# Part of the second feed-forward product in seven block products instead of eight (Strassen's scheme)

## The chip, the cores and the metric

One Trainium2 chip, one core. The metric is the device time of one execution in microseconds (us). The kernel before has a median of 726.84 us over 3 runs (726.24 to 728.11).

## What is computed

A transformer block over 512 tokens of width 1024, all in float32: four gated branches, an output product, and a feed-forward part. The change touches only the last of these:

```python
h = rmsnorm(x, norm_ffn_pre[l])
f = jnp.square(jax.nn.relu(h @ w_ff1[l])) @ w_ff2[l]
x = x + rmsnorm(f, norm_ffn_post[l])
```

`w_ff1` is 1024 x 4096, `w_ff2` is 4096 x 1024. The second product therefore sums over 32 K tiles of 128 for each of 4 token tiles of 128 and each of 2 column halves of 512.

## The kernel before, in words

**Three matmuls for one.** Each operand of a float32 product is split in a high part, rounded to the engine's fp32r form, and a low part, the remainder. `mm3` (L138) issues high x high, high x low and low x high. Every split costs one pass of ACT (the cast to the high part) and one of DVE (the subtraction that leaves the low part). `split_w` (L115) does so for a weight tile of 128 x 1024 and gives it one of five `wh`/`wl` buffers; `load` (L110) brings the raw tile over SP's queue into one of three `raw` buffers; `weights` (L135) is both. `split_by_dma` (L122) makes the low part without DVE: ACT writes the negated high part, and a DMA from POOL's queue adds the raw tile to it from memory.

**Order.** PE's instructions are kept in the order in which the program is written (`InOrder`, L85 to L102). For the other engines and the DMA queues the framework's planner chooses the order before the run, from the order of the program and from when it expects operands and buffers. A buffer that a pool reuses makes its next writer wait for its last reader (`reuse_waits="tile"`: tile by tile, also where one pool takes the memory of another that was closed).

**First feed-forward product.** It is already done in seven block products per pair of K tiles: `seven_w` (L337) makes the weight sums, `seven` (L351) issues seven `part`s of 12 matmuls of 256 columns into banks pa to pd, `forms` (L385) are the halves and sums of `h`. The loop at L1003 runs over the pairs j = 4, 6, ... 30. `finish` (L971) squares the relu into `u[j]` and splits it (`usplit`, L950, three buffers).

**Second product, left column half.** Inside that loop `second()` (L963) takes a finished K tile from `pend` and adds it to the four banks `acc`: 12 matmuls of 512 columns. It stands once after the fifth of the seven parts, and once or more at the end of the iteration (`while pend`).

**Second product, right column half.** After the loop `acc2` is summed over all 32 K tiles (L1037 to L1049). The last `LAST` = 6 K tiles are split ahead into buffers of their own (`held`), and the tail (L1050) runs token tile by token tile: six K tiles, a square with its sum on ACT, `norm_scale`, three passes of DVE, and two output DMAs. The left half is scaled into `fo` before (L1028 to L1032), and `gpost` is loaded at L1026 into memory that the pools of `hs` (the halves and sums of `h`) held.

Of the kernel before, what the change touches and what calls it, by code (L numbers as in the profile page):

```python
# [10 lines left out]
F32 = mybir.dt.float32  # L11
F32R = mybir.dt.float32r
I32 = mybir.dt.int32
AF = mybir.ActivationFunctionType
ALU = mybir.AluOpType
# [3 lines left out]
P = 128  # L19
S = 512  # L20
NT = S // P
D = 1024
# [8 lines left out]
NFF = DFF // P  # L31
# [49 lines left out]
def build(ctx, tc, d, out):  # L81
    nc = tc.nc
    DVE, POOL = nc.vector, nc.gpsimd
# [18 lines left out]
    PE, ACT = InOrder(nc.tensor, True), InOrder(nc.scalar, False)  # L102

    def f(t):
        return t.bitcast(F32)
# [4 lines left out]
    def load(src, n=1024):  # L110
        raw = wp.tile([P, 1024], F32, tag="raw", name="raw", bufs=3)
        nc.sync.dma_start(raw[:, :n], src)
        return raw

    def split_w(raw, n=1024):  # L115
        hi = wp.tile([P, 1024], F32R, tag="wh", name="wh", bufs=5)
        lo = wp.tile([P, 1024], F32R, tag="wl", name="wl", bufs=5)
        ACT.copy(hi[:, :n], raw[:, :n])
        DVE.tensor_tensor(lo[:, :n], raw[:, :n], f(hi)[:, :n], ALU.subtract)  # L119
        return hi, lo  # L120

    def split_by_dma(src, raw=None, n=1024, own=None):  # L122

        raw = load(src, n) if raw is None else raw
        if own is None:
            hi = wp.tile([P, 1024], F32R, tag="wh", name="wh", bufs=5)
            lo = wp.tile([P, 1024], F32R, tag="wl", name="wl", bufs=5)
        else:
            hi, lo = [own.tile([P, 1024], F32R, tag=f"b{c}", name=f"b{c}", bufs=1) for c in "hl"]
        ACT.copy(hi[:, :n], raw[:, :n])  # L130
        ACT.activation(lo[:, :n], f(hi)[:, :n], AF.Copy, scale=-1.0)
        POOL.dma_start(lo[:, :n], src.bitcast(F32R), accum_op=ALU.add)
        return hi, lo

    def weights(src, n=1024):  # L135
        return split_w(load(src, n), n)

    def mm3(ps, lhs, rhs, start, stop, more=False):  # L138

        k = dict(skip_group_check=more)  # L140
        PE.matmul(ps, lhs[0], rhs[0], start=start, stop=False, **k)
        PE.matmul(ps, lhs[0], rhs[1], start=False, stop=False, **k)
        PE.matmul(ps, lhs[1], rhs[0], start=False, stop=stop, **k)

    def sl(pair, *ix):
        return pair[0][ix], pair[1][ix]
# [39 lines left out]
    def bank(name):  # L186
        return mm.tile([P, 512], F32, tag="mm", name=name)
# [96 lines left out]
    for (a, b), xt, wa in zip(groups, xts, was):  # L284
        if a == 1:
            angles = rope_tables()
        for k in range(a, b):
# [11 lines left out]
            for i, (zz, ww) in enumerate(((zh, wah), (zl, wah), (zh, wal))):  # L299
                for t in range(NT):  # L300
                    PE.matmul(psA[t][:, :NA], zz[:, k, t * P:(t + 1) * P], ww[:, k, :],
                              start=k == 0 and i == 0, stop=k == KD - 1 and i == 2)
# [34 lines left out]
    def seven_w(srcs, by_dma):  # L337

        left, rght = load(srcs[0]), load(srcs[1])
        w = split_w(left)  # L340
        w22 = split_by_dma(srcs[1][:, B2], rght[:, B2], 512) if by_dma else split_w(rght[:, B2], 512)

        DVE.tensor_tensor(left[:, B1], rght[:, B1], left[:, B1], ALU.subtract)
        DVE.tensor_tensor(rght[:, B1], rght[:, B2], rght[:, B1], ALU.subtract)
        DVE.tensor_tensor(rght[:, B2], rght[:, B2], left[:, B1], ALU.subtract)
        DVE.tensor_tensor(left[:, B2], left[:, B2], rght[:, B2], ALU.subtract)
        yield w, w22
        yield split_w(left)
        yield split_w(rght)

    def seven(ws_, forms, small, g, h):  # L351

        A11, A12, A22, S1, S2, S3, S4 = forms
        (w, w22), wl, wr = ws_
        pa, pb = bank("pa"), bank("pb")
        part(pa, w, 0, A11, True)
        x1 = small()
        ACT.copy(x1, pa[:, :HS])
        yield
        part(pb, w, 512, A12, True)  # L360
        DVE.tensor_tensor(g[:, :HS], pb[:, :HS], x1, ALU.add)
        yield
        pc = bank("pc")
        part(pc, wl, 0, S1, True)
        x5 = small()
        ACT.copy(x5, pc[:, :HS])
        yield
        part(pa, wr, 512, S2, False)
        x2 = small()
        ACT.copy(x2, pa[:, :HS])  # L370
        yield
        pd = bank("pd")
        part(pd, wl, 512, A22, True)
        yield
        part(pc, w22, 0, S4, False)
        DVE.tensor_tensor(h[:, :HS], pc[:, :HS], x2, ALU.add)
        yield
        part(pa, wr, 0, S3, False)
        x3 = small()
        ACT.copy(x3, pa[:, :HS])  # L380
        DVE.tensor_tensor(g[:, HS:], pd[:, :HS], x3, ALU.add)  # L381
        DVE.tensor_tensor(h[:, HS:], x3, x5, ALU.add)
        yield
# [556 lines left out]

    up = ctx.enter_context(tc.tile_pool(name="up", bufs=1, reuse_waits="tile", **right))

    u = [up.tile([P, S], F32, name=f"u{j}") for j in reversed(range(NFF))][::-1]
    sst = up.tile([P, TOP], F32, name="sst")[:, :4 * NT].rearrange("p (t c) -> p t c", c=4)
    us = ctx.enter_context(tc.tile_pool(name="us", bufs=3, reuse_waits="tile", **right))
    acc = [bank("acc") for _ in range(NT)]

    pend = []

    def usplit(j):  # L950
        uh = us.tile([P, S], F32R, tag="uh", name="uh")
        ul = us.tile([P, S], F32R, tag="ul", name="ul")
        ACT.copy(uh, u[j])
        DVE.tensor_tensor(ul, u[j], f(uh), ALU.subtract)  # L954
        return uh, ul

    def ff2(dst, j, w, us_, t, first=0, last=NFF - 1):
        mm3(dst[t], sl(us_, slice(None), slice(t * P, (t + 1) * P)), sl(w, slice(None), slice((j % 2) * 512, (j % 2 + 1) * 512)),
            j == first, j == last)

    w2 = {0: weights(d["w2"][0, 0])}

    def second():  # L963

        j, us_ = pend.pop(0)
        if j and j % 2 == 0:
            w2[0] = weights(d["w2"][0, j // 2])
        for t in range(NT):
            ff2(acc, j, w2[0], us_, t)

    def finish(j):  # L971
        ACT.activation(u[j], u[j], AF.Relu)
        ACT.activation(u[j], u[j], AF.Square)
        pend.append((j, usplit(j)))

    first = seven_w((d["w1"][EARLY], d["w1"][EARLY + 1]), False)
    first_w = [next(first)]
# [24 lines left out]
    ops = forms(h2, hsum)  # L1002
    for j in range(EARLY, NFF, 2):  # L1003
        g, h = u[j], u[j + 1]
        for n, _ in enumerate(seven(first_w if j == EARLY else list(seven_w((d["w1"][j], d["w1"][j + 1]), False)),
                                      ops, small, g, h)):
            if n == 4 or n in (1, 2) and j == EARLY:
                second()
        while pend:
            second()  # L1010
        if j == NFF - 2:
            ahead_u = usplit(0)
        finish(j)
        finish(j + 1)

    acc2 = [bank("acc2") for _ in range(NT)]
    w = weights(d["w2"][1, 0])
    for t in range(NT):
        ff2(acc2, 0, w, ahead_u, t)
    while pend:  # L1020
        second()
    hs.close()

    lp = ctx.enter_context(tc.tile_pool(name="lp", bufs=1, reuse_waits="tile"))
    gpost = lp.tile([P, D], F32, name="gpost")
    nc.sync.dma_start(gpost, d["gpost"].partition_broadcast(P))  # L1026
    fo = lp.tile([P, NT, 512], F32, name="fo")
    for t in range(NT):  # L1028
        sq = lp.tile([P, S], F32, tag="r", name="r", bufs=2)
        ACT.activation(sq, acc[t], AF.Square, scale=r2[:, t:t + 1], accum_out=sst[:, t, 0:1])  # L1030
        DVE.tensor_scalar(sst[:, t, 0:1], sst[:, t, 0:1], D * EPS, None, ALU.add)
        DVE.scalar_tensor_tensor(fo[:, t, :], acc[t], r2[:, t:t + 1], gpost[:, :512], ALU.mult, ALU.mult)  # L1032


    LAST = 6
    held = []
    for j in range(1, NFF):  # L1037
        if j % 2 == 0:
            w = weights(d["w2"][1, j // 2])
        us_ = usplit(j) if j < NFF - LAST else None  # L1040
        if us_ is None:
            uh = lp.tile([P, S], F32R, name=f"luh{j}")
            ul = lp.tile([P, S], F32R, name=f"lul{j}")
            ACT.copy(uh, u[j])
            DVE.tensor_tensor(ul, u[j], f(uh), ALU.subtract)
            held.append((j, w, (uh, ul)))
        else:
            for t in range(NT):
                ff2(acc2, j, w, us_, t)  # L1049
    for t in range(NT):  # L1050
        for j, w, us_ in held:
            ff2(acc2, j, w, us_, t)
        sq = lp.tile([P, S], F32, tag="r", name="r", bufs=2)
        f2 = lp.tile([P, D], F32, tag="f2", name="f2", bufs=2)
        ACT.activation(sq, acc2[t], AF.Square, scale=r2[:, t:t + 1], accum_out=sst[:, t, 1:2])
        norm_scale(sst[:, t, 2:3], sst[:, t, 3:4], sst[:, t, 0:1], sst[:, t, 1:2])
        DVE.scalar_tensor_tensor(f2[:, 512:], acc2[t], r2[:, t:t + 1], gpost[:, 512:], ALU.mult, ALU.mult)
        DVE.scalar_tensor_tensor(f2[:, :512], fo[:, t, :], sst[:, t, 2:3], x1[:, t, :512], ALU.mult, ALU.add)
        nc.sync.dma_start(out[t * P:(t + 1) * P, :512], f2[:, :512])
        DVE.scalar_tensor_tensor(f2[:, 512:], f2[:, 512:], sst[:, t, 2:3], x1[:, t, 512:], ALU.mult, ALU.add)  # L1060
        nc.sync.dma_start(out[t * P:(t + 1) * P, 512:], f2[:, 512:])
# [78 lines left out]
```

## Time and profile before

| | |
|---|---|
| median of 3 runs | 726.84 us (726.24 to 728.11) |
| the profiled execution, its own time | 727.39 us |
| its span in the trace | 725.7 us |
| granted TensorE clock, mean | 0.999 of 2.4 GHz |
| gates' stage (seven-product form, accumulating DMAs) | 215 to 331 us |
| loop of the first feed-forward product | 406 to 623 us |
| rest of the second product | 623 to 719 us |
| last output | 719 to 726 us |

The profile names the engines PE (TensorE matmul), PEld (weight loads, beside PE), DVE (VectorE), ACT (ScalarE), POOL (GpSimd) and SP (the queue of most DMAs). A busy time is the sum of the instructions' durations. A row of a group reads: line, engine, operation, output <- inputs, form, count | busy us, mean ns | idle time of the engine just before, and who ended it. The chain of waits goes back from the last instruction, at each step to what released it.

### The profile page before, as it was taken

The numbers are of one execution on the slowest core, as the hardware profiler recorded it, in microseconds if no ns is written. First come the engines' busy times: TensorE is split into PE (matmuls) and PEld (weight loads), VectorE is DVE, ScalarE is ACT, GpSimd is POOL, SyncE is SP. The second block draws the span as 40 slices with busy tenths as digits, with TensorE's granted clock in tenths as the row PEclk, the third lists the DMA queues.
The fourth block names the chain that finished last, engine by engine and source line by source line (L and its number), as shares of the span: only waits on it lengthen the run. The fifth ranks groups of instructions, "written<-read, shape, count | busy, mean of one in ns | idle before, by whom it ended". The sixth has DMA issues, their size and how long they took to land.

```text
span 725.7 us, 11480 instructions
## 1 busy us (share of the span) xinstructions
PE 715.5 (99%) x4490; PEld 646.0 (89%) x4490; DVE 532.4 (73%) x887; ACT 405.6 (56%) x681; POOL 31.4 (4%) x49
## 2 busy tenths in 40 slices
PE   8999999999999999999999999999999999999996
PEld 7998788888999999998889999999999999888885
DVE  7599986994788988887368977766776767764515
ACT  6875444564556666663446754656555566744411
POOL 1110000000100100100011000000000000000001
PEclk9999999999999999999999999999999999999999
DMA  8533221242447646658424133233332332633103
GB/s 305 192 111 117 88 88 59 88 117 73 114 108 187 141 113 154 148 158 295 135 68 143 59 112 92 89 122 112 93 111 89 108 121 91 203 102 102 59 1 116
DMA packets 26182, 86.71 MB, mean 119 GB/s; under 512 B 3344, under 2 KB 3856, under 8 KB 26128
## 3 DMA queue, kind: packets, MB, share of 16 engines
q1 hardware_dynamic: 23072, 78.12, 32.6%
q0 software_dynamic: 3056, 7.87, 6.5%
q8 instruction: 35, 0.57, 0.3%
q14 instruction: 19, 0.16, 0.1%
HBM read 83.87 MB, written 2.10 MB: 118 GB/s over the span
## 4 chain that ended last, share of the span: by engine, by line
PE 95%; DVE 3%; DMA 1%; issue 0%; SPq 0%; ACT 0%; DVEq 0%; ACTq 0%
PE acc L95 24%; PE pa L95 15%; PE fb L95 12%; PE pc L95 10%; PE y L95 6%; PE wo L95 6%; PE pb L95 5%; PE pd L95 5%; PE z L95 3%; PE psA L95 2%; PE sgv L95 2%; PE po L95 1%; DMA wA<-in_wA 1%; PE tr L95 1%; PE s L95 1%; PE q L95 1%
## 5 line engine op out<-in xcount | busy, mean ns | idle before, releaser
L95 ACT CAST wh<-raw 128x1024 fp32r<-128x1024 f32 (+2 forms) x171 | 165.8, 981 | 142.2 <-PE pc L95 54.9
L119 DVE TENSOR_TENSOR wl<-raw,wh 128x1024 fp32r<-128x1024 f32 (+2 forms) x157 | 181.8, 1169 | 34.8 <-ACT wh L95 32.5
L95 PE MATMUL acc<-wh,uh 128*128 128x512 f32 x232 | 90.6, 391 | 0.0
L95 PE MATMUL acc<-wl,uh 128*128 128x512 f32 x232 | 90.6, 391 | 0.0
L95 PE MATMUL acc<-wh,ul 128*128 128x512 f32 x232 | 90.4, 390 | 0.0
L954 DVE TENSOR_TENSOR ul<-u,uh 128x512 fp32r<-128x512 f32 x58 | 38.7, 689 | 58.2 <-ACT uh L95 58.2
L95 PE MATMUL fb<-zh,wh 128*128 128x512 f32 x144 | 56.7, 394 | 0.1
L95 PE MATMUL fb<-zl,wh 128*128 128x512 f32 x144 | 56.1, 390 | 0.0
L95 PE MATMUL fb<-zh,wl 128*128 128x512 f32 x144 | 56.1, 390 | 0.0
L95 ACT CAST uh<-u 128x512 fp32r<-128x512 f32 x58 | 34.2, 617 | 33.9 <-PE acc L95 33.7
L95 PEld LDWEIGHTS acc<-wh,ul 128*128 128x128 f32 x232 | 43.6, 188 | 9.8 <-DVE ul L954 0.4
L95 PEld LDWEIGHTS acc<-wh,uh 128*128 128x128 f32 x232 | 43.6, 188 | 8.7 <-ACT uh L95 0.4
L95 PEld LDWEIGHTS acc<-wl,uh 128*128 128x128 f32 x232 | 43.5, 188 | 7.8
L95 ACT ACTIVATE u<-u 128x512 f32<-128x512 f32 x60 | 33.1, 621 | 17.7 <-DVE u L381 17.7
L95 ACT COPY x<-pa 128x256 f32<-128x256 f32 x78 | 28.6, 367 | 9.9 <-PE pa L95 8.3
L95 PEld LDWEIGHTS fb<-zh,wl 128*128 128x128 f32 x144 | 27.0, 188 | 5.8
L95 PEld LDWEIGHTS fb<-zh,wh 128*128 128x128 f32 x144 | 27.1, 188 | 5.7 <-DVE zc L434 0.4
L95 PEld LDWEIGHTS fb<-zl,wh 128*128 128x128 f32 x144 | 27.1, 188 | 5.3
L95 PE MATMUL pa<-hsh,wh 128*128 128x256 f32 x112 | 31.2, 279 | 0.0
L95 PE MATMUL pa<-hsl,wh 128*128 128x256 f32 x112 | 31.2, 279 | 0.0
L95 PE MATMUL pa<-hsh,wl 128*128 128x256 f32 x112 | 31.2, 279 | 0.0
L95 ACT ACTIVATE g<-g,c 128x512 f32<-128x512 f32 x32 | 22.5, 720 | 9.7 <-DVE g L821 9.7
(391 smaller groups left out, 1995.0 us busy)
## 6 DMA issues: line engine op xcount, KB each, us to landing
raw<-in_w SPq DMA_DIRECT2D x64, 512.0 KB, 3.5
raw<-in_wG SPq DMA_DIRECT2D x32, 512.0 KB, 3.6
raw<-in_wF SPq DMA_DIRECT2D x10, 512.0 KB, 3.6
raw<-in_wB SPq DMA_DIRECT2D x8, 512.0 KB, 4.8
raw<-in_wO SPq DMA_DIRECT2D x8, 512.0 KB, 4.5
bl<-in_wB POOLq DMA_DIRECT2D x7, 512.0 KB, 7.7
wl<-in_wG POOLq DMA_DIRECT2D x12, 256.0 KB, 4.3
xk<-in_x SPq DMA_DIRECT2D x4, 512.0 KB, 8.6
```

What stands on the lines that cost most here:

```text
L95: ins = op(*a, **k)
L119: DVE.tensor_tensor(lo[:, :n], raw[:, :n], f(hi)[:, :n], ALU.subtract)
L954: DVE.tensor_tensor(ul, u[j], f(uh), ALU.subtract)
```

## The change

K tiles 20 to 31 leave the plain sum and are taken in three rounds of two pairs each: round m combines the pairs `K0[m]` (tiles 20 to 25) and `K1[m]` (26 to 31), the halves of the tokens (`TA`, `TB`) and the column halves. The seven products of a round are spread over three places: four in the left half (A11 B11 into `pa`; A12 B21 into `acc[:2]`; S1 T1 into `pc`; A22 T4 into `acc[2:]`), two in the right half (S2 T2 into `pa`; A22' with S4 into `pc`), and one near the end (S3 T3 into `pa`). `pc` goes on as the first half of `acc2`. Partial results are copied to `fix` and added at the end. Each round loads its weight tiles anew in each place; sums of weights and of tokens are made by DVE, and split.

In the loop of the first product only one `second()` is left per iteration, `todo` holds K tiles until one of two places in `pend` is free, and `seven_w` is called with its accumulating form (True). K tiles 0 to 15 are added in the loop, 16 to 19 (`KEEP`) during the left rounds. The `u` tiles are allocated in pairs. The pool `qp` (raw tiles, token halves) and later `ep` (the `held` buffers) lie in memory that was `hs`'s.

```diff
+    pairs_u = [up.tile([P, 2, S], F32, name=f"u{j}") for j in reversed(range(NFF // 2))][::-1]
+    u = [pairs_u[j // 2][:, j % 2, :] for j in range(NFF)]
...
+    DUOS = 3
+    WHOLE = NFF - 4 * DUOS
+    KEEP = 4
+    pend, todo = [], []
+
+    def refill():
+        while todo and len(pend) < 2:
+            j = todo.pop(0)
+            pend.append((j, usplit(j)))
...
-            ff2(acc, j, w2[0], us_, t)
+            ff2(acc, j, w2[0], us_, t, j == 0, j >= WHOLE - KEEP - 1, j >= WHOLE - KEEP)
+        refill()
...
-        pend.append((j, usplit(j)))
+        if j < WHOLE:
+            todo.append(j)
+            refill()
...
-        for n, _ in enumerate(seven(first_w if j == EARLY else list(seven_w((d["w1"][j], d["w1"][j + 1]), False)),
+        for n, _ in enumerate(seven(first_w if j == EARLY else list(seven_w((d["w1"][j], d["w1"][j + 1]), True)),
...
-        while pend:
-            second()
...
+    def temp():
+        return lp.tile([P, S], F32, tag="r", name="r", bufs=4)
...
+    def loadq(src):
+        raw = qp.tile([P, 1024], F32, tag="raw", name="rawq", bufs=3)
+        nc.sync.dma_start(raw, src)
+        return raw
+
+    def halves_of(v):
+
+        a, b = [qp.tile([P, S], F32R, tag=f"a{c}", name=f"a{c}", bufs=5) for c in "hl"]
+        ACT.copy(two(a), v)
+        DVE.tensor_tensor(two(b), v, f(two(a)), ALU.subtract)
+        return two(a), two(b)
+
+    def block(dst, a, w, first):
+
+        for k in range(2):
+            for t in range(2):
+                mm3(dst[t], sl(a(k), slice(None), slice(t * P, (t + 1) * P)), sl(w, slice(None), slice(k * 512, (k + 1) * 512)),
+                    first and k == 0, k == 1, not first)
...
+    for m in range(DUOS):
+        last = m == DUOS - 1
+        u0, u1 = K0[m], K1[m]
+        b11, b12 = load(d["w2"][0, c0_ + m]), load(d["w2"][1, c0_ + m])
+        w11 = split_by_dma(d["w2"][0, c0_ + m], b11) if m else split_w(b11)
+        DVE.tensor_tensor(b11, b12, b11, ALU.subtract)
+        a11 = halves_of(u0[:, :, TA])
+        for _ in range(1 if m else 2):
+            second()
+        block(pa, of(a11), w11, m == 0)
...
+        b21, b22 = loadq(d["w2"][0, c1_ + m]), loadq(d["w2"][1, c1_ + m])
+        w21 = split_by_dma(d["w2"][0, c1_ + m], b21) if m else split_w(b21)
+        both = [halves_of(two(u1[:, k, :])) for k in range(2)]
...
+        block(acc[:2], lambda k: flat(k, TA), w21, False)
...
+        wt1 = split_w(b11)
+        v = temp()
+        DVE.tensor_tensor(two(v), u0[:, :, TB], u1[:, :, TB], ALU.add)
+        s1_ = halves_of(two(v))
+        block(pc, of(s1_), wt1, m == 0)
...
+        DVE.tensor_tensor(b22, b22, b11, ALU.subtract)
+        DVE.tensor_tensor(b21, b21, b22, ALU.subtract)
+        wt4 = split_w(b21)
+        block(acc[2:], lambda k: flat(k, TB), wt4, False)
...
+    for m in range(DUOS):
+        u0, u1 = K0[m], K1[m]
+        for _ in range(3 if m < 2 else 2):
+            third()
+        b11, b12 = load(d["w2"][0, c0_ + m]), load(d["w2"][1, c0_ + m])
+        b22 = loadq(d["w2"][1, c1_ + m])
+        DVE.tensor_tensor(b11, b12, b11, ALU.subtract)
+        DVE.tensor_tensor(b11, b22, b11, ALU.subtract)
+        wt2 = split_w(b11)
...
+        s2_ = halves_of(two(v))
+        block(pa, of(s2_), wt2, False)
+        w22 = split_by_dma(d["w2"][1, c1_ + m], b22)
...
+        s4_ = halves_of(two(v4))
+        block(pc, of(s4_), w22, False)
...
+    for m in range(DUOS):
+        u0 = K0[m]
+        for _ in range(2):
+            third()
...
+        DVE.tensor_tensor(b12, b22, b12, ALU.subtract)
+        wt3 = split_w(b12)
...
+        block(pa, of(s3_), wt3, False)
+    qs.close()
...
+        DVE.tensor_tensor(fix[:, 2 + t, :], fix[:, 2 + t, :], v, ALU.add)
+        DVE.tensor_tensor(v, acc[2 + t], v, ALU.add)
+        left_out(2 + t, v)
...
-        ACT.activation(sq, acc2[t], AF.Square, scale=r2[:, t:t + 1], accum_out=sst[:, t, 1:2])
+        DVE.tensor_tensor(v, acc2[t], fix[:, t, :], ALU.add)
+        ACT.activation(sq, v, AF.Square, scale=r2[:, t:t + 1], accum_out=sst[:, t, 1:2])
```

`third()` adds one K tile to the four banks of `acc2`: a `usplit`, a w2 tile for every second K tile, and 12 matmuls. `left_out` is the old scaling of the left half (square on ACT, scaling into `fo` on DVE).

## Rows read from the trace of the kernel before

**Rows 1.** The page's first part: busy us, share of the span, instructions.

```profile
PE 715.5 (99%) x4490; PEld 646.0 (89%) x4490; DVE 532.4 (73%) x887; ACT 405.6 (56%) x681; POOL 31.4 (4%) x49
```

**Rows 2.** The chain that ended last, from 595 us: start us, us, what.

```profile
595.47 1.40 PE pa L95 x12
...
610.76 1.40 PE pa L95 x12
...
623.31 95.81 PE acc L95 x420
```

**Rows 3.** Timeline of PE from 699 us: start us, us, instruction.

```profile
699.68 0.39 PE L95 MATMUL acc<-wh,ul 128*128 128x512 f32 x1
699.91 0.39 PE L95 MATMUL acc<-wh,uh 128*128 128x512 f32 x1
```

**Rows 4.** Engines by stage: window, us, busy of each, granted clock, DMA share, GB/s.

```profile
215.00:331.00 116.00, 116.00 (x881) 111.60 (x880) 101.63 (x153) 73.55 (x114) 11.14 (x13) 1.00 0.60 150
427.00:623.00 196.00, 196.00 (x1393) 183.65 (x1392) 137.62 (x191) 116.82 (x194) 0.00 (x0) 1.00 0.34 109
```

**Rows 5.** DVE's and ACT's groups by form, 427 to 623 us.

```profile
L119 DVE TENSOR_TENSOR wl<-raw,wh 128x1024 fp32r<-128x1024 f32 x52 | 62.7, 1224 | 11.3 <-ACT wh L95 9.9
L954 DVE TENSOR_TENSOR ul<-u,uh 128x512 fp32r<-128x512 f32 x27 | 17.5, 689 | 31.7 <-ACT uh L95 31.7
L344 DVE TENSOR_TENSOR raw<-raw 128x512 f32<-128x512 f32 x12 | 8.3, 692 | 0.4
L119 DVE TENSOR_TENSOR wl<-raw,wh 128x512 fp32r<-128x512 f32 x12 | 8.2, 684 | 0.0
L361 DVE TENSOR_TENSOR u<-pb,x 128x256 f32<-128x256 f32 x13 | 5.4, 418 | 0.0
...
L95 ACT CAST wh<-raw 128x1024 fp32r<-128x1024 f32 x52 | 53.5, 1050 | 50.2 <-PE pc L95 45.4 <-PE pa L95 4.2 <-PE pd L95 0.6
L95 ACT ACTIVATE u<-u 128x512 f32<-128x512 f32 x52 | 28.5, 619 | 17.7 <-DVE u L381 17.7
L95 ACT COPY x<-pa 128x256 f32<-128x256 f32 x38 | 13.9, 366 | 1.4
```

**Rows 6.** DMA from 427 to 702 us: queue, packets, MB, share; issues, landing of raw.

```profile
q1 hardware_dynamic: 7746, 28.19, 31.8%
...
raw<-in_w SPq DMA_DIRECT2D x52, 512.0 KB, 3.5
...
DMA to landing us min/median/max: 3.3/3.5/5.5
```

**Rows 7.** The same view from 215 to 331 us, the gates' stage.

```profile
q0 software_dynamic: 1909, 4.77, 24.4%
...
bl<-in_wB POOLq DMA_DIRECT2D x5, 512.0 KB, 7.8
...
wl<-in_wG POOLq DMA_DIRECT2D x8, 256.0 KB, 4.3
```

**Rows 8.** Accumulating DMAs of 512 KB by tile, bl and (360 to 400 us) wl.

```profile
L95 ACT ACTIVATE bl<-bh x7: 1051/1064/1065, 152.6 to 320.9; 128x1024 fp32r<-128x1024 f32 x7
L132 POOL DMA_DIRECT2D bl<-in_wB x7: 847/854/912, 153.9 to 322.3; - x7
...
DMA to landing us min/median/max: 6.9/7.7/9.1
...
L132 POOL DMA_DIRECT2D wl<-in_w x2: 857/870/884, 362.8 to 381.0; - x2
...
DMA to landing us min/median/max: 6.3/6.8/7.2
```

**Rows 9.** The chain that ended last, its end.

```profile
719.12 0.02 issue
...
719.21 0.69 ACT r L95
...
720.15 0.74 DVE f L1057
```

More of the change, by code (lines that the diff above doesn't have):

```diff
@@ L941, in build @@
     up = ctx.enter_context(tc.tile_pool(name="up", bufs=1, reuse_waits="tile", **right))
-    u = [up.tile([P, S], F32, name=f"u{j}") for j in reversed(range(NFF))][::-1]
+    pairs_u = [up.tile([P, 2, S], F32, name=f"u{j}") for j in reversed(range(NFF // 2))][::-1]
+    u = [pairs_u[j // 2][:, j % 2, :] for j in range(NFF)]
     sst = up.tile([P, TOP], F32, name="sst")[:, :4 * NT].rearrange("p (t c) -> p t c", c=4)
@@ L946, in build @@
     acc = [bank("acc") for _ in range(NT)]
-    pend = []
+    DUOS = 3
[6 more added lines that the diff above has]
+            pend.append((j, usplit(j)))
     def usplit(j):
@@ L955, in usplit, with ff2 @@
         return uh, ul
-    def ff2(dst, j, w, us_, t, first=0, last=NFF - 1):
+    def ff2(dst, j, w, us_, t, start, stop, more=False):
         mm3(dst[t], sl(us_, slice(None), slice(t * P, (t + 1) * P)), sl(w, slice(None), slice((j % 2) * 512, (j % 2 + 1) * 512)),
-            j == first, j == last)
+            start, stop, more)
     w2 = {0: weights(d["w2"][0, 0])}
@@ L1008, in build @@
                 second()
-        while pend:
-            second()
-        if j == NFF - 2:
-            ahead_u = usplit(0)
         finish(j)
         finish(j + 1)
[L1016 to L1021, printed above, removed]
+    K0 = pairs_u[WHOLE // 2:WHOLE // 2 + DUOS]
+    K1 = pairs_u[WHOLE // 2 + DUOS:]
+    c0_, c1_ = WHOLE // 2, WHOLE // 2 + DUOS
+    TA, TB = slice(0, HS), slice(HS, S)
     hs.close()
@@ L1027, in build @@
     fo = lp.tile([P, NT, 512], F32, name="fo")
-    for t in range(NT):
-        sq = lp.tile([P, S], F32, tag="r", name="r", bufs=2)
-        ACT.activation(sq, acc[t], AF.Square, scale=r2[:, t:t + 1], accum_out=sst[:, t, 0:1])
-        DVE.tensor_scalar(sst[:, t, 0:1], sst[:, t, 0:1], D * EPS, None, ALU.add)
-        DVE.scalar_tensor_tensor(fo[:, t, :], acc[t], r2[:, t:t + 1], gpost[:, :512], ALU.mult, ALU.mult)
-    LAST = 6
+    fix = lp.tile([P, NT, 512], F32, name="fix")
+    def temp():
+        return lp.tile([P, S], F32, tag="r", name="r", bufs=4)
@@ new lines, in left_out, with two @@
+    def left_out(t, src):
+        ACT.activation(temp(), src, AF.Square, scale=r2[:, t:t + 1], accum_out=sst[:, t, 0:1])
+        DVE.tensor_scalar(sst[:, t, 0:1], sst[:, t, 0:1], D * EPS, None, ALU.add)
+        DVE.scalar_tensor_tensor(fo[:, t, :], src, r2[:, t:t + 1], gpost[:, :512], ALU.mult, ALU.mult)
+    qs = ExitStack()
+    qp = qs.enter_context(tc.tile_pool(name="qp", bufs=1, reuse_waits="tile"))
+    def two(x):
+        return x.rearrange("p (k t) -> p k t", k=2)
+    def loadq(src):
+        raw = qp.tile([P, 1024], F32, tag="raw", name="rawq", bufs=3)
+        nc.sync.dma_start(raw, src)
+        return raw
@@ new lines, in of, with flat @@
+    def of(pair):
+        return lambda k: sl(pair, slice(None), k)
+    pa, pc = ([bank(n) for _ in range(2)] for n in ("qa", "qc"))
+    for m in range(DUOS):
[8 more added lines that the diff above has]
+        block(pa, of(a11), w11, m == 0)
+        if last:
+            x1s = [temp() for _ in range(2)]
+            for t in range(2):
+                ACT.copy(x1s[t], pa[t])
+        b21, b22 = loadq(d["w2"][0, c1_ + m]), loadq(d["w2"][1, c1_ + m])
+        w21 = split_by_dma(d["w2"][0, c1_ + m], b21) if m else split_w(b21)
+        both = [halves_of(two(u1[:, k, :])) for k in range(2)]
+        def flat(k, ts):
+            return [x.rearrange("p k t -> p (k t)")[:, ts] for x in both[k]]
+        block(acc[:2], lambda k: flat(k, TA), w21, False)
+        if last:
+            for t in range(2):
+                DVE.tensor_tensor(x1s[t], acc[t], x1s[t], ALU.add)
+        wt1 = split_w(b11)
[3 more added lines that the diff above has]
+        block(pc, of(s1_), wt1, m == 0)
+        if last:
+            for t in range(2):
+                ACT.copy(fix[:, 2 + t, :], pc[t])
+        DVE.tensor_tensor(b22, b22, b11, ALU.subtract)
+        DVE.tensor_tensor(b21, b21, b22, ALU.subtract)
+        wt4 = split_w(b21)
+        block(acc[2:], lambda k: flat(k, TB), wt4, False)
@@ new lines, in build, with third @@
+    for t in range(2):
+        left_out(t, x1s[t])
+    LAST = 6
+    acc2 = pc + [bank("acc2") for _ in range(2)]
+    wr2 = {}
+    todo.extend(range(WHOLE))
+    def third():
+        j = todo.pop(0)
+        if j % 2 == 0:
+            wr2[0] = weights(d["w2"][1, j // 2])
+        us_ = usplit(j)
+        for t in range(NT):
+            ff2(acc2, j, wr2[0], us_, t, j == 0 and t >= 2, True, j > 0 or t < 2)
+    for m in range(DUOS):
[7 more added lines that the diff above has]
+        wt2 = split_w(b11)
+        v = temp()
+        DVE.tensor_tensor(two(v), u0[:, :, TB], u1[:, :, TB], ALU.add)
+        DVE.tensor_tensor(two(v), two(v), u0[:, :, TA], ALU.subtract)
+        s2_ = halves_of(two(v))
+        block(pa, of(s2_), wt2, False)
+        w22 = split_by_dma(d["w2"][1, c1_ + m], b22)
+        v4 = temp()
+        DVE.tensor_tensor(two(v4), u1[:, :, TA], two(v), ALU.subtract)
+        s4_ = halves_of(two(v4))
+        block(pc, of(s4_), w22, False)
@@ new lines, in build @@
+    for t in range(2):
+        ACT.copy(fix[:, t, :], pa[t])
+    for m in range(DUOS):
+        u0 = K0[m]
+        for _ in range(2):
+            third()
+        b12, b22 = load(d["w2"][1, c0_ + m]), loadq(d["w2"][1, c1_ + m])
+        DVE.tensor_tensor(b12, b22, b12, ALU.subtract)
+        wt3 = split_w(b12)
+        v = temp()
+        DVE.tensor_tensor(two(v), u0[:, :, TA], u0[:, :, TB], ALU.subtract)
+        s3_ = halves_of(two(v))
+        block(pa, of(s3_), wt3, False)
+    qs.close()
@@ L1036, in build @@
+    ep = ctx.enter_context(tc.tile_pool(name="ep", bufs=1, reuse_waits="tile"))
+    for t in range(2):
+        v = temp()
+        ACT.copy(v, pa[t])
+        DVE.tensor_tensor(fix[:, 2 + t, :], fix[:, 2 + t, :], v, ALU.add)
+        DVE.tensor_tensor(v, acc[2 + t], v, ALU.add)
+        left_out(2 + t, v)
     held = []
-    for j in range(1, NFF):
+    while todo:
+        j = todo.pop(0)
         if j % 2 == 0:
[L1039 to L1049, printed above, removed]
+            wr2[0] = weights(d["w2"][1, j // 2])
+        uh = ep.tile([P, S], F32R, name=f"luh{j}")
+        ul = ep.tile([P, S], F32R, name=f"lul{j}")
+        ACT.copy(uh, u[j])
+        DVE.tensor_tensor(ul, u[j], f(uh), ALU.subtract)
+        held.append((j, wr2[0], (uh, ul)))
@@ L1050, in build @@
     for t in range(NT):
         for j, w, us_ in held:
-            ff2(acc2, j, w, us_, t)
-        sq = lp.tile([P, S], F32, tag="r", name="r", bufs=2)
-        f2 = lp.tile([P, D], F32, tag="f2", name="f2", bufs=2)
-        ACT.activation(sq, acc2[t], AF.Square, scale=r2[:, t:t + 1], accum_out=sst[:, t, 1:2])
+            ff2(acc2, j, w, us_, t, False, j == WHOLE - 1, True)
+        v, sq = temp(), temp()
+        f2 = ep.tile([P, D], F32, tag="f2", name="f2", bufs=2)
+        DVE.tensor_tensor(v, acc2[t], fix[:, t, :], ALU.add)
@@ L1056, in build @@
+        ACT.activation(sq, v, AF.Square, scale=r2[:, t:t + 1], accum_out=sst[:, t, 1:2])
         norm_scale(sst[:, t, 2:3], sst[:, t, 3:4], sst[:, t, 0:1], sst[:, t, 1:2])
-        DVE.scalar_tensor_tensor(f2[:, 512:], acc2[t], r2[:, t:t + 1], gpost[:, 512:], ALU.mult, ALU.mult)
+        DVE.scalar_tensor_tensor(f2[:, 512:], v, r2[:, t:t + 1], gpost[:, 512:], ALU.mult, ALU.mult)
         DVE.scalar_tensor_tensor(f2[:, :512], fo[:, t, :], sst[:, t, 2:3], x1[:, t, :512], ALU.mult, ALU.add)
```

## Prediction

> **What bounds the kernel now.** I read the busy table of the page first: PE 715.5 of 725.7 us, no other engine above 73% [rows 1]. Then the chain that ended last: from 595 us on it is PE alone, block after block without a gap, and from 623.31 to 719.12 one piece of 420 products [rows 2]. So until 719 us the time is what PE is given to do; a change pays if it takes matmuls away and adds no wait. A matmul of 128x512 is listed at 0.39 us, but the next starts 0.23 us later [rows 3], so 0.39 is no price. The price is 95.81/420 = 0.2281 us [rows 2], and 12 of them (one block product, or one K tile over four token tiles) take 2.74 us. Third, the table by stage: PE is full in each, also in the gates' stage (215 to 331 us), where DVE is busy 101.63 of 116 us, 88% [rows 4]. That stage has the form that is copied here: seven products whose operands ACT and DVE make just ahead of PE. So DVE at 88% does not by itself stop PE.
>
> **Removed.** K tiles 20 to 31 cost 12 x 8 x 3 = 288 matmuls (12 K tiles, eight token-by-column tiles, three terms). Now they are three rounds of seven products of 12: 252. All have the old shape, one weight load each. 36 x 0.2281 = **8.21 us** off PE, 1.1% of the run. The other 20 K tiles keep their 480.
>
> **First feed-forward loop.** One `second()` stands in an iteration where two stood; the products return later, so PE's sum is unchanged, but an iteration shrinks from 15.29 us (595.47 to 610.76) [rows 2] to 12.55. Per iteration DVE then has 3 x 1.224 + 4 x 0.692 + 4 x 0.42 + 0.69 + half a 1.224 = 9.4 us and ACT 3.5 x 1.05 + 4 x 0.365 + 7 x 0.62 = 9.5 us [rows 5]: 75% each, below 88%. In 13 iterations w22's DVE subtract (0.684) becomes an ACT pass of 0.62 and an accumulating DMA of 256 KB on POOL's queue, 4.3 us to landing [rows 7]: 5.5 us in all, against an iteration between two uses of w22. Cost taken 0. If that cover went, each iteration would wait.
>
> **Work beside the 21 products** (a round is one m). Left half, later rounds, five products (13.7 us): DVE makes five and a half passes of 1024 columns (three sums, two splits, half of a w2 tile) and six of 512: 5.5 x 1.224 + 6 x 0.69 = 10.9 us, 79%. First round, six products (16.4 us): 8 x 1.224 + 7 x 0.69 = 14.6, 89%. Right half: 4.5 x 1.224 + 8 x 0.69 = 11.0 of 13.7, and 9.7 of 10.9 in the short round, 89%. Last part: 3 x 1.224 + 4 x 0.69 = 6.4 of 8.2. ACT stays under 75% (later left rounds: 6.5 x 1.05 + 5 x 0.62 = 9.9) [rows 5]. All are at or about the gates' 88%, so no throughput term; what can be late is a chain.
>
> Five chains, each with its cover. (1) The first left product waits for `hs` to come free, then for a11: 0.62 + 0.69 us, under two `second()` (5.5 us): 0. (2) Its b21 load lands 3.5 us after that (5.5 at most) [rows 6], plus 1.05 + 1.22 us of splitting, under three products (8.2 us): 0. SP issues gpost between; while it waits for `hs`, loads behind it wait, as gpost does already before, without a PE wait. (3) pc is copied out (two copies, 0.62 each) under one product of 2.74 us before the right half writes its bank again: 0. The accumulator banks come free two products ahead: 0. (4) The accumulating DMAs of the left half, and (5) the start of the tail, have a price.
>
> (4) In rounds 1 and 2, w11 and w21 are made by ACT cast, ACT negation and an accumulating DMA of 512 KB. ACT takes 1.05 + 1.06; landing took 6.9 to 9.1, median 7.7 [rows 8]: 9.8 us, with one ACT instruction in front and some of the spread about 11.5. A round takes four of the five wh/wl buffers and the w2 tile the fifth, so w21's buffer comes free after its product and is wanted four products later: 10.95 us. A wait for w21 gives the next w11 the same extra time, so one wait per round, not two: 2 x 0.55 = **1.1 us**. From both sides: 0 (landing in 6.9) and 2 x (9.1 + 2.1 + 2 x 1.05 - 10.95) = 4.7. I take the value near the median row, as seven transfers of just this kind gave it. The Trainium skill, "DMA: Bandwidth & Descriptors", section on the anatomy of a SWDGE DMA, fits such a DMA at 2.0 us plus bytes over 436 GB/s, an estimated 3.2 us here; by it the chain has no wait and the sum below is 1.1 us lower. The 7.7 us of the row is over twice that, and the row decides. The w22 of the right half needs two slots and a half of five per round: 0.
>
> (5) Six split K tiles (`held`) were ready long before the tail; now their buffers lie where `qp` was, and come free with its last uses. The first group of the tail eats one every 3 x 0.2281 = 0.68 us; DVE splits one in 0.69 [rows 5], with three w2 splits (1.22 each) and four adds and two scalings of the left half around the same time. If the splits are done early: 0. If the adds and scalings (4 x 0.69 + 2 x 0.74) all stand ahead: 4.2 us. I take one late split, **0.7 us**: five of six lie on buffers that are free before the last product.
>
> **The end.** Each token tile gets an add of `fix` on DVE ahead of the square; only the last counts. Today PE's last product leads to the square at 719.21 and the chain follows [rows 9]. The add is a 128x512 DVE pass, 0.69 to 0.74, and one more hand-over between engines, about 0.1: **+0.8 us**.
>
> **Sum**, against the profiled execution's own time (727.39 us; span 725.7, 1.7 around it): -8.21 + 1.1 + 0.7 + 0.8 = -5.6, so 721.8. It was 0.55 over the median of the runs, 726.84; from the median: **721.2 us**.
>
> **Rivals.** *A, the DMA engines are full in the left half.* A later round moves 4.5 raw loads and two accumulates. A 512 KB load takes 0.318 x 275 x 0.524/28.19 = 1.63 us of all 16 engines [rows 6]; an accumulate 0.244 x 116 x 0.524/4.77 = 3.1 [rows 7]: 13.5 us of 13.7. Then each accumulate lands one such transfer later (10.8), the chain is 14.0 with one ACT instruction, and the two waits are 6.1: -8.21 + 6.1 + 0.7 + 0.8 = -0.6, 726.2. For it: no stage of before is that dense (the gates' stage has a DMA share of 0.60 [rows 4]). Against: the first round has no accumulate, so raw loads can run ahead there. The rows bear it out weakly: 7.8 us to landing in the gates' stage [rows 7] against 6.8 with fewer loads about [rows 8]. The Trainium skill, "DMA: Bandwidth & Descriptors", section on queues, rings and completion order, says that each DMA engine takes turns between the queues that have work, so that a busy SP queue would about halve what POOL's gets. Chance 0.12.
>
> *B, slower: DVE is late once for each product.* PE runs in written order, and a DVE subtract that waits for a load or a product holds those behind it. Here each of 21 products takes freshly made operands on both sides. If one 512 pass (0.69) is late each time: 21 x 0.69 = 14.5, the time is 726.84 - 8.21 + 0.8 + 14.5 = 733.9. It decides from 9.6/21 = 0.46 us per product (8.21 - 0.8 + 2.2) for a slowdown by over 0.3%. For it: 79 to 89% of DVE over 107 us. Against: the gates' stage, full PE at 88% [rows 4]. Chance 0.09.
>
> *C, fewer products are not fewer matmuls.* The count above excludes it, unless the strided token halves slow the loads of weights; they are copied flat first. Within A and B.
>
> **How the numbers follow.** A measurement of this kernel tells about 0.3% (2.2 us) from no change. The forecast (all waits together under 5.2 us, so below 724.7) has 0.79, A 0.12 (no change), B 0.09. Bounds: no wait and the short add, -8.21 + 0.69, gives 719.3, with 0.6 of scatter of the runs 718.7. Both upper ends, 4.7 + 4.2 + 0.84 - 8.21, give +1.5, 728.4; that takes both at once, and A lies at 726.2, so the range ends at 727.2. The forecast alone: 718.7 to 724.6.
>
> **What would show it.** PE's busy time 8 us less; matmuls 36 fewer; PE without waits in the first loop at 12.55 us per iteration; in rounds 1 and 2 of the left half waits of PE for a DMA into wl of about half a us, twice; a first tail group with a wait under 1 us; from PE's last product to the end 0.8 us more. Wrong if PE waits on DVE again and again in the 107 us of products (B), if landing of the 512 KB accumulates goes beyond 10 us (A), or if the first loop shows waits.

## The result: slower, 735.56 us, and the profile after

The changed kernel takes 735.56 us (median of 4 runs, 734.74 to 736.17) against 726.98 for the kernel before (4 runs by then): ratio 1.0116, 95% interval 1.0098 to 1.0133. The forecast was 721.2 with a range of 718.7 to 727.2. The profiled execution has a span of 734.4 us, 8.7 over the 725.7 of before.

The page's first part of the changed kernel (busy us, share, instructions), against [rows 1]:

```profile
PE 712.6 (97%) x4454; PEld 640.9 (87%) x4454; DVE 558.5 (76%) x916; ACT 433.8 (59%) x715; POOL 48.4 (7%) x69
```

There are 36 matmuls fewer, as counted, but PE's busy time fell by 2.9 us, not 8.2, and its share by two points. So matmuls became slower in part, and PE waited. Where, say the engines by stage (window, us, then PE, PEld, DVE, ACT, POOL busy, granted clock, DMA share, GB/s):

```profile
423.31:585.00 161.69, 161.69 (x1238) 155.31 (x1238) 116.75 (x161) 113.42 (x189) 10.18 (x12) 1.00 0.46 126
587.80:705.00 117.20, 109.23 (x465) 88.60 (x464) 82.05 (x99) 65.32 (x89) 5.93 (x7) 0.97 0.63 190
705.40:714.00 8.60, 6.10 (x21) 3.16 (x20) 7.63 (x14) 5.73 (x12) 0.00 (x0) 1.00 0.00 0
```

The first feed-forward loop is full, as before [rows 4]. In the stretch of the products PE is idle for 8.0 us, in the first token tile of the tail for 2.5 more. Who ended PE's waits after 585 us (total us, times, longest):

```profile
PE qa L95 <- DMA wl<-in_w: 5.2, 1, 5.2
PE qc L95 <- DVE lul L1181: 2.0, 5, 0.8
PE acc L95 <- DMA wl<-in_w: 1.0, 1, 1.0
PE qc L95 <- DVE al L1061: 0.9, 1, 0.9
PE acc L95 <- DVE wl L119: 0.8, 1, 0.8
PE qc L95 <- ACT luh L95: 0.5, 1, 0.5
```

The longest is w11 of round 1, the first weight tile that an accumulating DMA makes. PE's timeline there:

```profile
608.19 0.39 PE L95 MATMUL qa<-wh,ah 128*128 128x512 f32 x1
613.75 0.79 PE L95 MATMUL qa<-wl,ah 128*128 128x512 f32 x1 [5.17 <-DMA wl<-in_w]
614.34 0.63 PE L95 MATMUL qa<-wh,al 128*128 128x512 f32 x1
614.77 0.63 PE L95 MATMUL qa<-wh,ah 128*128 128x512 f32 x1
...
619.46 0.47 PE L95 MATMUL acc<-wh,al 128*128 128x512 f32 x1
619.77 0.40 PE L95 MATMUL acc<-wh,ah 128*128 128x512 f32 x1
```

The product stopped after one matmul. When it went on, the next matmuls started 0.43 us apart where 0.23 is the rule [rows 3]: from 613.75 to 619.77 there are 14 steps, 6.02 us for 14 x 0.2281 = 3.19, so 2.8 us went on top of the wait. The view by stage shows the granted clock, first in a wider stretch, then in the slow matmuls alone:

```profile
614.00:630.00 16.00, 16.00 (x60) 12.93 (x61) 8.02 (x8) 7.42 (x9) 1.69 (x2) 0.82 0.79 218
...
614.30:619.40 5.10, 5.10 (x13) 3.95 (x12) 0.33 (x1) 0.98 (x2) 0.00 (x0) 0.50 0.95 313
```

The matmuls ran at a granted clock of 0.50, the lower of the two levels (1.2 GHz), after PE had stood still for over 5 us. The Trainium skill, "TensorE: Matmul & The Clock Gate", part 1, states that an idle spell throttles the array to half rate and activity releases it; the trace agrees, with 0.43 for 0.23 us. The 2.8 us are this execution's figure: after waits of 5.5 to 6.1 us at the same place in tail_qp, gpost_none and gpost_late, by the same measure, the slow matmuls cost 1.7 to 2.1.

The account against before, from the start-to-start times of the matmuls: the wait for w11 5.3; slow clock 2.8; three shorter waits of the left half 3.9 in all (at 602.8, 634.1 and 638.3 us); the tail's first token tile 4.2; from the start of PE's last matmul to the end of the span 8.1 against 7.0 us, 1.2 more. Together 17.4; less 8.2 saved, and less 0.5 because the matmuls of the products that did not wait started 0.2267 us apart and not 0.2281, 8.7 us. (A wait costs more than the idle time that the profile lists for it, w11's about 0.16: a matmul is listed 0.16 longer than its place. After the shorter waits the next matmul comes late as well, by 0.1.)

**Why w11 is late.** Here is ACT's timeline in the left half's round 0, of the changed kernel:

```profile
594.48 1.05 ACT L95 CAST wh<-raw 128x1024 fp32r<-128x1024 f32 x1
...
596.99 0.62 ACT L95 CAST uh<-u 128x512 fp32r<-128x512 f32 x1
600.48 1.05 ACT L95 CAST wh<-rawq 128x1024 fp32r<-128x1024 f32 x1 [2.87 <-DVE rawq L1110]
601.44 1.99 ACT L95 CAST wh<-raw 128x1024 fp32r<-128x1024 f32 x2
603.34 1.06 ACT L95 ACTIVATE wl<-wh 128x1024 fp32r<-128x1024 f32 x1
```

And the POOL queue's first two issues with, from the view by tile, the landing times of its seven accumulating DMAs from 585 us on:

```profile
604.69 0.84 POOL L132 DMA_DIRECT2D wl<-in_w  x1 [32.62 <-ACT wl L95]
607.10 0.85 POOL L132 DMA_DIRECT2D wl<-in_w  x1 [1.57 <-ACT wl L95]
...
DMA to landing us min/median/max: 5.6/8.4/10.4
```

ACT stood still for 2.87 us before the cast of wt4, whose sum DVE was still making; w11's cast (601.44) and negation (603.34) of the next round were queued behind it. So w11's DMA was issued at 604.69 and PE wanted its result at 608.4. It landed at 613.7, 9.0 us after the issue. The 2.87 us are only a part of the delay: the casts of wt4 and of a w2 tile stood ahead of the negation too, and hoist below shows w11's DMA issued 6.6 us earlier.

### The profile page after: what moved, and what is told of

Same layout as the page of the kernel before. It is cut to its first block, busy times and chain, and to the rows that moved or that the text cites. A ratio compares the mean times of both kernels' runs of the same rounds, so it can differ in the third digit from the quotient of the medians.

```text
span 734.4 us, 11549 instructions
## 1 busy us (share of the span) xinstructions
PE 712.6 (97%) x4454; PEld 640.9 (87%) x4454; DVE 558.5 (76%) x916; ACT 433.8 (59%) x715; POOL 48.4 (7%) x69
## 4 chain that ended last, share of the span: by engine, by line
PE 87%; DVE 5%; DMA 4%; issue 3%; ACT 1%; SPq 0%; DVEq 0%; POOLq 0%; POOL 0%; ACTq 0%
PE pa L95 15%; PE acc L95 11%; PE fb L95 10%; PE pc L95 10%; PE y L95 6%; PE wo L95 6%; PE pb L95 5%; PE pd L95 5%; PE qc L95 5%; PE z L95 3%; PE qa L95 3%; DMA wl<-in_w 3%; PE psA L95 2%; PE sgv L95 2%; PE po L95 1%
## 5 line engine op out<-in xcount | busy, mean ns | idle before, releaser
L119 DVE TENSOR_TENSOR wl<-raw,wh 128x1024 fp32r<-128x1024 f32 (+1 forms) x142 | 170.8, 1213 | 64.3 <-ACT wh L95 63.4
L95 PE MATMUL acc<-wl,uh 128*128 128x512 f32 x108 | 42.2, 391 | 0.0
L95 PE MATMUL acc<-wh,uh 128*128 128x512 f32 x108 | 42.2, 391 | 0.0
L95 PE MATMUL acc<-wh,ul 128*128 128x512 f32 x108 | 42.0, 389 | 0.0
L132 POOL DMA_DIRECT2D wl<-in_w x22 | 18.7, 851 | 309.0 <-ACT wl L95 219.0
L95 ACT CAST uh<-u 128x512 fp32r<-128x512 f32 x34 | 21.0, 620 | 27.3 <-PE acc L95 27.3
L965 DVE TENSOR_TENSOR ul<-u,uh 128x512 fp32r<-128x512 f32 x34 | 23.2, 688 | 5.6 <-ACT uh L95 5.4
L95 PE MATMUL pa<-zsh,wl 128*128 128x256 f32 x96 | 26.9, 280 | 0.0
L95 PE MATMUL pa<-zsh,wh 128*128 128x256 f32 x96 | 26.9, 280 | 0.0
```

Of the source, the lines that this page charges most:

```text
L95: ins = op(*a, **k)
```

## The experiments

Theory 1: the accumulating DMAs come too late, by the moment of their issue, and the long wait also costs the clock; the tail's splits are late because all stand behind the last product. Theory 2 is rival B, DVE late product by product. Theory 3 is rival A, landing in full DMA engines. Each kernel starts from the changed one; ratios are to the kernel before, with 95% intervals.

| run | median us | ratio to before |
|---|---|---|
| the change | 735.56 | 1.0116 [1.0098, 1.0133] |
| no_acc | 727.54 | 1.0002 [0.9993, 1.0011] |
| hoist | 729.48 | 1.0030 [1.0019, 1.0041] |
| gpost_late | 735.59 | 1.0111 [1.0094, 1.0128] |
| gpost_none | 734.82 | 1.0101 [1.0087, 1.0115] |
| tail_qp | 732.00 | 1.0065 [1.0050, 1.0080] |
| no_acc_tail | 723.63 | 0.9943 [0.9929, 0.9956] |
| no_fix | 722.55 | 0.9930 [0.9917, 0.9944] |
| best | 722.59 | 0.9931 [0.9918, 0.9943] |
| best2 | 723.21 | 0.9957 [0.9944, 0.9971] |
| hoist_tail | 723.70 | 0.9952 [0.9939, 0.9966] |
| loop_dve | 722.31 | 0.9940 [0.9926, 0.9954] |

The kernel before was run again beside each group: its median was 727.37 us beside no_acc, hoist, gpost_late and tail_qp, 727.37 beside gpost_none, no_acc_tail, no_fix and best, and 727.03 beside best2, hoist_tail and loop_dve. Kernels of different groups are better compared by their ratios.

**no_acc: without the accumulating DMAs of the left half.**

```diff
-        w11 = split_by_dma(d["w2"][0, c0_ + m], b11) if m else split_w(b11)
+        w11 = split_w(b11)
-        w21 = split_by_dma(d["w2"][0, c1_ + m], b21) if m else split_w(b21)
+        w21 = split_w(b21)
```

> w11 and w21 of the left half's rounds 1 and 2 are split by ACT and DVE as in round 0; the four accumulating DMAs of 512 KB are gone. Theory 1 (those DMAs come too late, and the wait also costs the clock): the waits of 5.2 and 1.0 us on wl and the slow matmuls after the first of them go, together some 9 us of the 735.6: 726 to 727. Theory 2 (DVE is late product by product, rival B): DVE gets 2.4 us more per round, 13.3 of 13.7, so PE waits at more products: 732 or more.

Measured: 727.54 us, 8.0 less, half a us over theory 1's figure and far below theory 2's. In the view by stage the clock is back and DVE is full:

```profile
601.00:614.00 13.00, 12.08 (x53) 9.44 (x52) 13.00 (x15) 8.24 (x11) 0.00 (x0) 1.00 0.73 222
614.00:630.00 16.00, 14.94 (x66) 11.89 (x64) 15.52 (x18) 10.15 (x14) 0.00 (x0) 1.00 0.72 230
```

DVE is busy 28.5 of 29 us and PE still loses only 2.0 there. So a full DVE does not stop PE product by product, and rival B is not the cause.

**hoist: the DMAs stay, w11 is issued earlier.**

```diff
         DVE.tensor_tensor(b22, b22, b11, ALU.subtract)
+        if not last:
+            b11, b12 = load(d["w2"][0, c0_ + m + 1]), load(d["w2"][1, c0_ + m + 1])
+            w11 = split_by_dma(d["w2"][0, c0_ + m + 1], b11)
         DVE.tensor_tensor(b21, b21, b22, ALU.subtract)
```

(The loads and the split at the head of the round are left to round 0.)

> The loads of b11 and b12 and the accumulating split of w11 for the next round are written ahead of this round's wt4, so ACT casts w11 before it waits for wt4's sum; all DMAs stay. If the lateness is that of the issue (ACT's order), w11 of round 1 is issued some 7 us earlier, its wait of 5.2 us and the slow clock go: 727 to 729. If it is the landing in full DMA engines, the wait moves to w21 or to round 2 and the time stays above 732.

Measured: 729.48 us, half a us over the figure for the issue. ACT's cast of w11, the POOL queue's first two issues, PE's longest waits from 595 to 645 us, and the engines from 605 to 620 us:

```profile
595.25 1.05 ACT L95 CAST wh<-raw 128x1024 fp32r<-128x1024 f32 x1
...
598.08 0.84 POOL L132 DMA_DIRECT2D wl<-in_w  x1 [26.27 <-DVE rawq L1110]
606.58 0.85 POOL L132 DMA_DIRECT2D wl<-in_w  x1 [7.65 <-DVE wl L119]
```

```profile
PE qc L95 <- DVE sst L1043: 1.5, 1, 1.5
PE acc L95 <- DMA wl<-in_w: 1.4, 1, 1.4
PE acc L95 <- DVE wl L119: 0.8, 1, 0.8
```

```profile
605.00:620.00 15.00, 13.58 (x61) 10.90 (x60) 9.97 (x12) 9.98 (x13) 2.55 (x3) 1.00 1.04 327
```

The issue is 6.6 us earlier, w11's wait and the slow clock are gone, and w21 of round 1 waits 1.4. The DMA engines are fuller than in the changed kernel (share 1.04), and yet this is 6.1 us faster: full engines alone do not make the loss.

One thing hoist does not separate. In the changed kernel w21 of round 1 was late too, hidden behind the wait for w11: it landed at 617.5, and without that wait PE would have wanted it at about 611.1 (an estimate: 13 matmuls after 608.19). In hoist it is issued only 0.5 us earlier, but lands much sooner. The view by tile of this one DMA, in the changed kernel and then in hoist:

```profile
L132 POOL DMA_DIRECT2D wl<-in_w x1: 853/853/853, 607.1 to 607.1; - x1
...
DMA to landing us min/median/max: 10.4/10.4/10.4
```

```profile
L132 POOL DMA_DIRECT2D wl<-in_w x1: 853/853/853, 606.6 to 606.6; - x1
...
DMA to landing us min/median/max: 5.9/5.9/5.9
```

So for w21 the gain is a shorter landing and not an earlier issue. In the changed kernel five raw loads and both accumulating DMAs of the round were issued between 603.9 and 610.9 us; in hoist w11's went out 8.5 us ahead of w21's. That this crowd made the landing long fits these times, but no run shows it by itself.

**gpost_late and gpost_none: less for the DMA engines to do.**

```diff
-    nc.sync.dma_start(gpost, d["gpost"].partition_broadcast(P))
...
+    nc.sync.dma_start(gpost, d["gpost"].partition_broadcast(P))
     for t in range(2):
         left_out(t, x1s[t])
```

> The 512 KB load of gpost moves from ahead of the left rounds to behind them, nothing else. If full DMA engines at the start of the left half set how late round 1's w11 is, the loads of b21 and b22 land 1 to 1.6 us sooner and the wait of 5.2 us shrinks by as much: 733 to 734.5. If only the order of ACT's work counts, no change: 735.5 within 0.5.

Measured: 735.59 us, no change, but it tells nothing of the load: the planner issued it at 586.97 us, where it had been at 586.44. So the load was taken out:

```diff
-    nc.sync.dma_start(gpost, d["gpost"].partition_broadcast(P))
+    POOL.memset(gpost, 1.0)
```

> The change as it is, but gpost is filled with ones by POOL instead of being loaded (the output leaves out that weight). The run with the load moved in the text issued it at the same moment, so it told nothing; this one takes its 512 KB away. If full DMA engines make round 1's w11 late, b21 and b22 land 1 to 1.6 us sooner, and the wait of 5.2 us shrinks by that: 733.5 to 734.5. If the order of ACT's work alone counts: 735.5.

Measured: 734.82 us; its interval overlaps that of the change. PE's longest wait in it:

```profile
PE qa L95 <- DMA wl<-in_w: 5.4, 1, 5.4
```

The wait is no shorter. The load of gpost has no part in it. It lies 18 us ahead of w11's DMA (586.44 against 604.69), so this says nothing of the raw loads that stand beside that DMA.

**tail_qp: other buffers for the held splits.**

```diff
-    qs.close()
-    ep = ctx.enter_context(tc.tile_pool(name="ep", bufs=1, reuse_waits="tile"))
...
-        uh = ep.tile([P, S], F32R, name=f"luh{j}")
-        ul = ep.tile([P, S], F32R, name=f"lul{j}")
+        if j < WHOLE - 5:
+            held.append((j, wr2[0], usplit(j)))
+            continue
+        uh, ul = [qp.tile([P, S], F32R, tag=f"a{c}", name=f"a{c}", bufs=5) for c in "hl"]
```

(`f2` takes buffers of `qp`'s raw tiles.)

> The six held splits of the tail take buffers of the pools us and qp (one and five), freed one by one, instead of a pool opened after qp is closed. If the tail's waits of about 3.8 us come from all six splits standing behind the last product in ACT's order, five now stand ahead of it: 732 (3 to 3.8 less). If they come from DVE having too much to do around the tail, the waits stay: 735 to 736.

Measured: 732.0 us, 3.6 less. ACT's timeline of the changed kernel shows the fault:

```profile
698.03 1.05 ACT L95 CAST wh<-raw 128x1024 fp32r<-128x1024 f32 x1 [1.67 <-PE qa L95]
705.47 0.59 ACT L95 COPY r<-qa 128x512 f32<-128x512 f32 x1 [6.39 <-PE qa L95]
705.95 1.66 ACT L95 CAST luh<-u 128x512 fp32r<-128x512 f32 x3
```

And the same place in tail_qp:

```profile
697.61 1.05 ACT L95 CAST wh<-raw 128x1024 fp32r<-128x1024 f32 x1
704.79 0.59 ACT L95 COPY r<-qa 128x512 f32<-128x512 f32 x1 [6.13 <-PE qa L95]
705.27 0.62 ACT L95 CAST ah<-u 128x512 fp32r<-128x512 f32 x1
```

ACT idles 6 us before the last product ends in both. In the changed kernel all six casts stand behind the copy of its result (three more follow at 708.73); in tail_qp one does, and PE's waits in the tail (4.2 us by the account above) are gone. Whether the new pool's buffers came free only then, or the planner only expected that, is not shown.

**no_acc_tail: both.** The edits of no_acc and tail_qp together.

> Both edits: w11 and w21 split by ACT and DVE in all left rounds, and the six held splits in buffers of us and qp. If the two waits are independent of each other, the tail's gain of 3.5 us comes on top of 727.5: 724.0, 0.4% under the kernel before. If DVE, which the left half now fills, pushes work into the tail, part of the gain is lost: 725.5 to 727.

Measured: 723.63 us, 0.57% under the kernel before. The two gains add up (8.0 and 3.6 of 11.9).

**no_fix: the price of the add at the end.**

```diff
-        DVE.tensor_tensor(v, acc2[t], fix[:, t, :], ALU.add)
-        ACT.activation(sq, v, AF.Square, scale=r2[:, t:t + 1], accum_out=sst[:, t, 1:2])
+        ACT.activation(sq, acc2[t], AF.Square, scale=r2[:, t:t + 1], accum_out=sst[:, t, 1:2])
```

(The scaling behind it reads `acc2[t]` as well.)

> As no_acc_tail, without the adds of fix in the last token-tile loop: the output leaves out the partial products that fix holds. It prices the add at the end. From PE's last product to the end the kernel of the change took 1.1 to 1.2 us more than the kernel before; if that is the add and its hand-over, 1.1 us less than no_acc_tail: 722.9. If it lies elsewhere, the same as no_acc_tail.

Measured: 722.55 us, 1.1 less than no_acc_tail, as forecast, but in part for another reason. In no_acc_tail DVE is still busy with the token tile before when PE ends, and the add starts 0.92 us after PE's last matmul starts; in the changed kernel it was 0.43 (726.26 to 726.69):

```profile
713.77 0.39 PE L95 MATMUL acc<-wh,al 128*128 128x512 f32 x1
...
714.69 0.68 DVE L1187 TENSOR_TENSOR r<-acc,fix 128x512 f32<-128x512 f32 x1
```

From the start of the last matmul to the end of the span the two traces differ by 1.25 us (8.62 and 7.37), and about 0.5 of that is this wait for DVE; the add and its hand-over are 0.78. tail_qp has the same 0.5 (8.60 us, where the changed kernel had 8.13), which is why it gained 3.6 and not 4.2.

**best: the collecting adds behind the next product's operand.**

```diff
-        if last:
-            for t in range(2):
-                DVE.tensor_tensor(x1s[t], acc[t], x1s[t], ALU.add)
         wt1 = split_w(b11)
...
         if last:
             for t in range(2):
                 ACT.copy(fix[:, 2 + t, :], pc[t])
+        if last:
+            for t in range(2):
+                DVE.tensor_tensor(x1s[t], acc[t], x1s[t], ALU.add)
```

> As no_acc_tail, and in the last left round the two adds that collect the finished left tiles are written behind the product that follows, so that DVE makes that product's operand first. The wait of 1.7 us before that product goes: 722.3 to 722.8. If DVE is full there anyway, the wait reappears at the next product: 724.

Measured: 722.59 us, 1.0 less than no_acc_tail, 0.69% under the kernel before. The runs of the two overlap (721.77 to 723.32 and 722.68 to 724.47), but the traces show the wait shorter, 0.4 us listed where no_acc_tail has 1.5. PE's waits after 585 us that are left:

```profile
PE acc L95 <- DVE wl L119: 0.8, 1, 0.8
PE qc L95 <- DVE al L1061: 0.4, 1, 0.4
```

**best2: one K tile moved ahead to cover the first of these.**

```diff
-        for _ in range(1 if m else 2):
+        for _ in range((2, 0, 1)[m]):
             second()
...
         wt4 = split_w(b21)
+        if m == 0:
+            second()
```

> As best, and round 1's K tile of the plain sum (12 matmuls, 2.7 us) is added in round 0 ahead of the product with wt4, whose low part came 1.3 us late in best. The wait is covered and goes: 721.2 to 721.6. If DVE, full in this stretch, only meets it later, round 1's first product waits instead: 722.6 as best.

Measured: 723.21 us, no gain, by the ratios 0.26% slower than best; the moved K tile itself waits, for its own w2 tile:

```profile
PE acc L95 <- DVE wl L119: 1.0, 1, 1.0
PE acc L95 <- ACT wh L95: 0.9, 1, 0.9
```

**hoist_tail: the DMAs kept, with everything else of best.** hoist, tail_qp and best's order of the adds.

> The accumulating DMAs stay, with w11 issued ahead (hoist) and the two edits of the tail and of the collecting adds from best. If the DMAs' only fault was the moment of issue, this is as fast as best, 722.6; if their landing in full DMA engines still costs waits (1.4 us on w21 and 0.4 on the right half's w22 in hoist), 724.3 to 725.

Measured: 723.70 us, between the two figures, 1.1 over best by the medians and 0.21% (1.5 us) by the ratios. What it has beyond best is above all w21's wait:

```profile
PE acc L95 <- DMA wl<-in_w: 1.4, 1, 1.4
...
PE acc L95 <- ACT wh L95: 0.5, 1, 0.5
```

**loop_dve: undo the loop's part.** best, with `False` for `True` in the loop's `seven_w`.

> As best, with w22 of the first feed-forward loop split by DVE again instead of the accumulating DMA of 256 KB. DVE then has 10.1 of 12.55 us per iteration, 81%. If that part of the change has no effect on the end, as forecast (cost 0 either way): 722.6 within 0.7. If DVE needs the room: PE waits in the loop and more than 724.

Measured: 722.31 us, as best within the spread of the runs. PE is full in the loop in both, with DVE at 124.74 of 164 us in place of 118.10:

```profile
423.00:587.00 164.00, 164.00 (x1258) 157.60 (x1258) 124.74 (x176) 105.64 (x177) 0.00 (x0) 1.00 0.33 107
```

## Why the prediction was wrong, step by step

- **Removed, 8.21 us: right.** 36 matmuls fewer at the old price; best, where most waits are gone, is 0.69% (5 us) under before even with the add at the end and two waits, 1.7 us together.
- **First feed-forward loop, 0: right.** An iteration takes 12.54 us (536.23 to 548.77 in the chain), without a wait, and loop_dve finds no effect of the new split.
- **Chain (4), 1.1 us: this failed, and with it the sign.** The step says that "w21's buffer comes free after its product and is wanted four products later: 10.95 us", and lets the work start when the buffer is free. In round 1 it did not. ACT's queue held w11's cast behind wt4's, and wt4's behind DVE's sum, so that w11's DMA was issued 6.6 us later than hoist shows possible. The wait was 5.3 us, for w11; w21 was late as well, hidden behind it. The landing of 7.7 us was too short too: 8.4 to 10.4 in the left half. In round 2 the step held but for that landing. ACT took up w21 at 622.02, as soon as a product of PE released it, and PE wanted the tile 10.9 us later; its landing of 9.6 us made the wait, 1.2 us where the step has 0.55.
- **No term for the clock.** A wait of 5 us was priced at 5 us. It cost 2.8 more in slow matmuls.
- **Chain (5), 0.7 us: mis-sized, at its upper end.** That "five of six lie on buffers that are free before the last product" was no statement of when they are written: none of the six was cast before it. It is the same error as in chain (4). They cost 4.2 us, the bound itself.
- **No throughput term: right**, and by a wide margin: in no_acc DVE is full for 29 us. What it left out is the order within DVE's and ACT's queues. Two waits of some 1.2 us each (wt4 in round 0, the operand behind the collecting adds in round 2) had no price; best halves the second.
- **The end, 0.8 us: right for the add.** The square starts 1.22 us after the start of the last matmul, where it was 0.49: 0.73 more. The whole end took 1.2 more; the other 0.4 lie behind the issue of the last output (3.76 us to the end of the span, 3.36 before).
- **Rivals.** B's figure, 733.9, was near the result but its mechanism was not: PE waited once for long, not at each of 21 products. That its figure came near was luck. A's landing was right in part (8.4 to 10.4 us in the left half, for 7.7; the prediction's sign for A was a landing beyond 10), but hoist has fuller engines and is faster. The 3.2 us of the fit that the prediction took from the Trainium skill, "DMA: Bandwidth & Descriptors", section on the anatomy of a SWDGE DMA, is far below every accumulating DMA of 512 KB from 585 us on (5.6 at least); the page's fit says nothing of accumulating ones.

Two waits in best (0.8 and 0.4 us listed) stay open; so does by how much the crowd of raw loads and accumulating DMAs lengthens a landing, as no run held the issue fixed and changed the loads beside it.

## What to carry to other kernels

Where PE bounds, price a change's removed matmuls, and then look for the work of the next step that the engines' queues hold behind a waiting instruction: a buffer that is free and an engine that is idle do not mean that the work has begun. Here a chain with a slow accumulating DMA at its end was better issued ahead of the instruction that waits (hoist), and better still made by DVE, even though DVE was then full (no_acc). Where a group of buffers takes the memory of a pool that was just closed, look whether the work that fills them was planned behind that pool's last user, as the six splits of the tail were.

## What was not expected of the hardware

- After PE had waited 5.2 us, the next 14 steps between matmuls took 6.0 us, most of them 0.43 in place of 0.23, at the lower clock level; after waits of at most 1.6 us (no_acc, hoist) the granted clock stayed at 1.00.
- DVE busy 28.5 of 29 us ahead of a PE that loses 2.0 us: a full engine fed PE nearly without loss.
- In the changed kernel an accumulating DMA of 512 KB took up to 10.4 us to land beside raw loads and another of its kind, and 5.6 at best.
